# 32 of 48 blocks of modulations as row sums on VectorE, instead of float32 matmuls and products by feature tile

## The chip, the cores and the metric

One core of a Trainium2 chip runs the whole network. The metric is the device time of one execution in microseconds (us), the median of the runs shown.

## What is computed

Two residual layers over 256 latent and 256 context tokens of 1024 features. Layer 0 mixes tokens by neighbourhood attention and a gated linear recurrence (HGRN2), layer 1 by an SSD recurrence; each mixer is followed by a convolutional FFN of width 2816. What the change touches is the modulation: two vectors, `silu(c)` for the latent and `silu(c_ctx)` for the context tokens, times a 1024 x 6144 matrix in each layer.

```python
s_lat = jax.nn.silu(c)
s_ctx = jax.nn.silu(c_ctx)[None]
for l in range(DEPTH):
    sh_m, sc_m, g_m, sh_f, sc_f, g_f = jnp.split(s_lat @ w_mod[l] + b_mod[l], 6, axis=-1)
    csh_m, csc_m, cg_m, csh_f, csc_f, cg_f = jnp.split(s_ctx @ w_mod[l] + b_mod[l], 6, axis=-1)
    u = modulate(h, norm_mix[l], sh_m, sc_m)      # rms_norm * (1 + scale) + shift
    ...
    h = h + g_m[:, None] * y
    h = h + g_f[:, None] * conv_ffn(modulate(h, norm_ffn[l], sh_f, sc_f), ffn_w_up[l],
                                    ffn_conv_w[l], ffn_conv_b[l], ffn_w_down[l])
```

So per layer there are six chunks of 1024 columns: 0 shift and 1 scale of the mixer's norm, 2 the mixer's gate, 3 and 4 shift and scale of the FFN's norm, 5 the FFN's gate. Everything is float32.

## The kernel before

Features lie on partitions (8 tiles of 128), the 512 tokens on the free axis. Every large product is made of three float32r matmuls: `wsplit` (L127) loads a weight of 512 KB on SyncE's queue, ScalarE casts its high part (`whi`, L136) and VectorE subtracts it for the low part (`wlo`, L138), four buffers of each; `mm3` (L142, L145) multiplies high by low, high by high and low by high; `proj` and `proj_tm` (L147, L153) loop over the 8 feature tiles. A scheduler in the framework writes the order of each engine from the program order, the tiles and its own costs; each engine then runs its list strictly in order.

**Modulations.** The 2 x 6 x 1024 columns are made in 48 blocks of 256. `mod_load` (L168) fetches a block's 1 MB, `mod_block` (L173) multiplies it by both vectors in 8 float32 matmuls (16 records, L181), up to four blocks sharing a bank of PSUM; `mod_finish` (L190) copies the bank (`mrow`, L187), transposes it back to features on partitions (L193), adds up four column groups (L195), and `mod_store` (L198) adds the bias (L204) and, for scales, makes `A = (1 + scale) * gain` (L207). `bg` (L222) puts the next block into TensorE's stream between two projections; three blocks are loaded ahead.

16 of the 48 blocks take another way, within FFN 0: `vec_half` (L232) multiplies half a block, feature tile by feature tile, by a scalar per partition on VectorE and adds into `vacc` (L247, L249; 16 instructions of 128x256 for a block, 8 for each vector), and `vec_flush` (L256) has TensorE add up the partitions of four blocks with a ones-matmul (L264), ScalarE copy the sums (L267) and TensorE transpose them (L270).

**Where the blocks stand.** 8 at the start, for layer 0's first norm (L720, L731); 12 queued at L482 and put between the projections of the two HGRN pairs (L485, L500); one behind the attention (L766) and 3 in FFN 0's norm (`norm_mod`, L371); 16 on VectorE in FFN 0 (L420, L439); one late in FFN 0 (L441), 3 in layer 1's norm, one behind the SSD groups (L789), 3 in FFN 1's norm.

**Around the change.** `hybrid` (L714 on) starts with the projection of the first outputs, feature tile by feature tile, as modulations arrive: for tile k, VectorE normalises (`nt`, L364), ScalarE modulates and rounds (`xhi`, L366), VectorE makes the rest (`xlo`, L367). Meanwhile small parameters load on ScalarE's queue, among them `lbx` (L449), from which the bounds of the forget gates are made on VectorE (L451 to L461). `hgrn_pair` then projects the queries, forget gates and values of a pair of heads, and works through halving levels of its decay products on VectorE (L514), each with many small matmuls on TensorE (L536, into `attc` by L538 and L543). Pair 1's levels run beside the attention's first projections (L162 to L164).

Of the kernel before, what the change touches and what calls it, by code (L numbers as in the profile page):

```python
# [16 lines left out]
P = 128  # L17
# [9 lines left out]
BATCH = 4  # L27
# [7 lines left out]
def mod_cols(g, kt):  # L35
    """The two 128-column blocks of w_mod that block kt of group g makes."""
    if g == 0:
        return kt, 8 + kt
    if g == 2:
        return 24 + kt, 32 + kt  # L40
    i = (16 if kt < 4 else 40) + 2 * (kt % 4)
    return i, i + 1


class Net:
    def __init__(self, tc, ctx, ins, out):
# [32 lines left out]
        self.half, self.vdone = 0, None  # L79
# [11 lines left out]
    def act_set(self, n, after):  # L91
        """Loads a table set on the scalar engine, behind one of its instructions."""
# [23 lines left out]
    def open_psum(self, start):  # L116
        """Three banks: one for modulations and two at the start, shared later."""
# [8 lines left out]
    # ---------------------------------------------------------------- weights  # L126
# [39 lines left out]
    # ------------------------------------------------------------ modulations  # L166
    # groups: 0 shift and scale of the mixer, 1 the two gates, 2 shift and scale of the ffn
    def mod_load(self, l, g, k0, n, m, pool=None, bufs=3):  # L168
        w = (pool or self.w).tile([P, NK, 2 * P], F32, tag="wm", bufs=bufs, name=self.nm("wm"))
        self.nc.sync.dma_start(w, self.i["wmod"][l, g, k0 + m])  # L170
        return w, l, g, k0, n, m

    def mod_block(self, w, l, g, k0, n, m):  # L173
        """Block k0 + m of group g, the m-th of n that share a bank of PSUM; the last one finishes all n."""
# [4 lines left out]
        for k in range(NK):  # L179
            j = k % 4  # L180
            mm = nc.tensor.matmul(ps[32 * j:32 * j + 32, :2 * P], self.silu_c[:, k, 6 - 2 * m:38 - 2 * m], w[:, k, :],  # L181
                                  start=(m == 0 and k < 4), stop=(m == n - 1 and k >= 4))
# [28 lines left out]
    def queue(self, batches):  # L211
        self.pending += [(l, g, k0, BATCH, m) for l, g, k0 in batches for m in range(BATCH)]
        self.fetch()

    def fetch(self):
        while self.pending and len(self.loaded) < 3:
            self.loaded.append(self.mod_load(*self.pending.pop(0)))
# [14 lines left out]
    def vec_half(self, pool):  # L232
        """Half of a block's products on the vector engine; the tensor engine adds up the partitions of n blocks."""
        nc = self.nc
        self.vec_flush()
        if not self.loaded and not self.half:
            return
        if not self.half:
            self.vw = self.loaded.pop(0)
            if self.vw[-1] == 0:  # L240
                self.vacc = pool.tile([P, self.vw[-2], 2, 2 * P], F32, tag="vacc", bufs=1, name=self.nm("vacc"))
        w, l, g, k0, n, m = self.vw
        for k in range(4 * self.half, 4 * self.half + 4):
            for s in STREAMS:
                acc, sc = self.vacc[:, m, s], self.silu_c[:, k, 6 + s:7 + s]
                if k == 0:
                    nc.vector.tensor_scalar(out=acc, in0=w[:, k], scalar1=sc, scalar2=None, op0=ALU.mult)  # L247
                else:
                    nc.vector.scalar_tensor_tensor(out=acc, in0=w[:, k], scalar=sc, in1=acc, op0=ALU.mult, op1=ALU.add)  # L249
        if self.half:  # L250
            self.fetch()
            if m == n - 1:
                self.vdone = (self.vacc, l, g, k0, n, pool)
        self.half = 1 - self.half

    def vec_flush(self):  # L256
        if not self.vdone:
            return
        nc = self.nc
        acc, l, g, k0, n, pool = self.vdone  # L260
        self.vdone = None
        ps = self.ps_b()
        for m in range(n):
            nc.tensor.matmul(ps[32 * m:32 * m + 32], self.ones[:, :32], acc[:, m].rearrange("p s c -> p (s c)"),  # L264
                             start=True, stop=True)
        rows = pool.tile([P, T], F32, tag="vrow", bufs=1, name=self.nm("vrow"))
        nc.scalar.copy(rows, ps)  # L267
        pt = self.ps_b()
        for i in range(4):
            nc.tensor.transpose(pt[:, i * P:(i + 1) * P], rows[:, i * P:(i + 1) * P], self.ident)  # L270
        self.mod_store(cust(pt, 0, [[P, 2], [32, n], [2 * P, 2]]), l, g, k0, n)
# [4 lines left out]
    # ------------------------------------------------------------------- norm  # L276
# [4 lines left out]
    def rsqrt_few(self, y, x, n, pool):  # L281
        """y = 1 / sqrt(x / n + eps) for a few columns: Newton steps on the vector engine."""
# [12 lines left out]
    def sumsq(self, k, tok):  # L295
        """Adds the squares of feature tile k to the running sum over the features."""
# [12 lines left out]
    def norm_r(self, ps, t0, n, meanwhile):  # L309
        """1 / rms of each token, on every partition; the sums go to ps."""  # L310
# [24 lines left out]
    def first_norm(self, p, meanwhile):  # L335
        """Loads the tokens; 1 / rms of each, on every partition."""
# [20 lines left out]
    def norm_u(self, l, which, k, r, xhi, xlo, streams, pool):  # L357
        """Feature tile k of the modulated norm, in two parts."""
# [12 lines left out]
    def norm_mod(self, l, which, xhi, xlo, streams, pool):  # L371
        self.bg(1, self.last_mm)
        r = self.norm_r(self.ps_s(), S * streams[0], S * len(streams), lambda i: self.bg(1, i))
        self.vec_flush()
# [27 lines left out]
    # -------------------------------------------------------------------- ffn  # L402
# [715 lines left out]
```

## Time and profile before

| | |
|---|---|
| median of 3 runs | 1255.38 us (1254.75 to 1260.44) |
| profiled execution, first to last instruction (span) | 1254.5 us |
| time around the span, median less span | 0.9 us |
| mean granted TensorE clock | 0.998 |
| busy share: TensorE, VectorE, ScalarE | 98%, 70%, 47% |
| all transfers | 188 MB, 150 GB/s on average |

The page gives the profiled execution by its span alone. PE is TensorE, DVE VectorE, ACT ScalarE, SP SyncE. A line L181 is line 181 of the kernel before; the changed kernel has its own line numbers. "Idle before" is the time an engine stood before an instruction and what released it. Matmuls overlap on TensorE, so a group's busy time there is more than what it adds to the span.

### The profile page before, as it was taken

What the parts mean: (1) busy time and instruction counts of PE and PEld (TensorE: products, weight loads), DVE (VectorE), ACT (ScalarE), POOL (GpSimd) and SP (SyncE); (2) the same over time, 40 slices, a digit from 0 to 9 for tenths busy, and PEclk for the clock granted to TensorE, in tenths of its full rate; (3) what the DMA queues carried; (4) which work ended last, traced back from release to release, by engine and by line L of the source; (5) the groups of instructions that cost most, each with busy time, mean ns of one, the idle gap of its engine ahead of it and who ended that gap; (6) DMA issues with size and microseconds to landing.
All of it is one profiled execution on the core that took longest, in us unless ns stands there. A gap on an engine that the chain in (4) does not pass through costs nothing.

```text
span 1254.5 us, 19641 instructions
## 1 busy us (share of the span) xinstructions
PE 1225.9 (98%) x7827; PEld 991.1 (79%) x7827; DVE 874.7 (70%) x1599; ACT 589.3 (47%) x918; POOL 0.2 (0%) x4
## 2 busy tenths in 40 slices
PE   5899999999999999999999999999999999999998
PEld 4686787766677887887887887777777798999998
DVE  5558257477658969647849747688989786766665
ACT  4364434678645332233223335646473644645452
POOL 0000000000000000000000000000000000000000
PEclk9999999999999999999999999999999999999999
DMA  9744552223044544433634444445343345565663
GB/s 377 255 140 150 185 206 65 69 78 118 21 138 165 179 157 153 166 99 94 212 102 161 142 146 151 143 133 181 110 159 118 101 154 167 171 186 180 187 181 106
DMA packets 49195, 188.34 MB, mean 150 GB/s; under 512 B 6480, under 2 KB 10192, under 8 KB 42832
## 3 DMA queue, kind: packets, MB, share of 16 engines
q1 hardware_dynamic: 46224, 185.17, 44.4%
q10 hardware_dynamic: 2880, 1.92, 0.5%
q8 instruction: 61, 1.00, 0.3%
q14 instruction: 30, 0.25, 0.1%
HBM read 185.95 MB, written 1.11 MB: 149 GB/s over the span
## 4 chain that ended last, share of the span: by engine, by line
PE 92%; DVE 3%; DMA 2%; ACT 1%; issue 1%; ACTq 0%; SPq 0%; DVEq 0%
PE a L145 54%; PE s L145 17%; PE b L181 1%; PE b L699 1%; PE s L162 1%; PE s L163 1%; PE s L164 1%; PE b L998 1%; PE b L993 1%; PE s L679 1%; PE b L693 1%; PE s L680 1%; PE b L966 1%; PE b L931 1%; DMA bcB<-cum_scratch 1%
## 5 line engine op out<-in xcount | busy, mean ns | idle before, releaser
L136 ACT CAST whi<-raw 128x1024 fp32r<-128x1024 f32 (+1 forms) x234 | 240.8, 1032 | 363.0 <-PE a L145 281.8
L138 DVE TENSOR_TENSOR wlo<-raw,whi 128x1024 fp32r<-128x1024 f32 (+1 forms) x234 | 280.4, 1200 | 137.9 <-ACT whi L136 136.7
L145 PE MATMUL a<-xhi,wlo 128*128 128x512 f32 (+1 forms) x740 | 271.2, 371 | 0.6 <-ACT va L634 0.3
L145 PE MATMUL a<-xhi,whi 128*128 128x512 f32 (+1 forms) x740 | 271.0, 366 | 0.0
L145 PE MATMUL a<-xlo,whi 128*128 128x512 f32 (+1 forms) x740 | 258.1, 366 | 1.0 <-DVE xlo L367 1.0
L145 PEld LDWEIGHTS a<-xhi,wlo 128*128 128x128 f32 x740 | 138.9, 188 | 32.1 <-issue 6.0
L145 PEld LDWEIGHTS a<-xlo,whi 128*128 128x128 f32 x740 | 137.3, 188 | 28.9 <-issue 4.8
L145 PEld LDWEIGHTS a<-xhi,whi 128*128 128x128 f32 x740 | 139.3, 188 | 24.5 <-issue 2.9
L145 PE MATMUL s<-xhi,wlo 128*128 128x512 f32 (+1 forms) x376 | 128.5, 342 | 0.0
L145 PE MATMUL s<-xhi,whi 128*128 128x512 f32 (+1 forms) x376 | 128.0, 340 | 0.0
L145 PE MATMUL s<-xlo,whi 128*128 128x512 f32 (+1 forms) x376 | 121.9, 342 | 0.0
L145 PE MATMUL a<-hh,whi 128*128 128x256 f32 (+1 forms) x359 | 119.5, 333 | 0.0
L145 PE MATMUL a<-hh,wlo 128*128 128x256 f32 (+1 forms) x359 | 112.9, 334 | 0.0
L145 PE MATMUL a<-hl,whi 128*128 128x256 f32 (+1 forms) x359 | 111.7, 334 | 0.0
L249 DVE SCALAR_TENSOR_TENSOR vacc<-wm,silu_c,vacc 128x256 f32<-128x256 f32 x224 | 93.1, 477 | 0.0
L381 DVE SCALAR_TENSOR_TENSOR h<-a,modT,h 128x256 f32<-128x256 f32 x90 | 40.7, 480 | 62.5 <-PE a L145 62.5
L145 PEld LDWEIGHTS s<-xhi,wlo 128*128 128x128 f32 x376 | 70.6, 188 | 9.7 <-issue 0.4
L145 PEld LDWEIGHTS s<-xhi,whi 128*128 128x128 f32 x376 | 70.7, 188 | 9.1
L145 PEld LDWEIGHTS s<-xlo,whi 128*128 128x128 f32 x376 | 69.3, 188 | 9.1
L145 PEld LDWEIGHTS a<-hh,whi 128*128 128x128 f32 x359 | 68.2, 190 | 6.6
L145 PEld LDWEIGHTS a<-hh,wlo 128*128 128x128 f32 x359 | 66.6, 190 | 7.7 <-DVE t L424 0.8
L145 PEld LDWEIGHTS a<-hl,whi 128*128 128x128 f32 x359 | 66.3, 190 | 7.0
(340 smaller groups left out, 1827.6 us busy)
## 6 DMA issues: line engine op xcount, KB each, us to landing
wm<-in_wmod SPq DMA_DIRECT2D x48, 1024.0 KB, 5.6
raw<-in_wup SPq DMA_DIRECT2D x88, 512.0 KB, 4.1
raw<-in_win SPq DMA_DIRECT2D x41, 512.0 KB, 3.7
raw<-in_wdn SPq DMA_DIRECT2D x32, 448.0 KB, 3.3
raw<-in_wo SPq DMA_DIRECT2D x24, 512.0 KB, 3.7
raw<-in_wdn SPq DMA_DIRECT2D x16, 512.0 KB, 3.6
raw<-in_wz SPq DMA_DIRECT2D x16, 512.0 KB, 3.9
mix<-cum_scratch SPq DMA_DIRECT2D x8, 512.0 KB, 4.7
```

The costliest lines, as they stand in the source:

```text
L136: nc.scalar.copy(hi, raw)
L138: nc.vector.tensor_tensor(out=lo, in0=raw, in1=hi.bitcast(F32), op=ALU.subtract)
L145: self.last_mm = self.nc.tensor.matmul(ps, w, x, start=(first and i == 0), stop=(last and i == 2))
L162: mm(ps, xhi[:, k, tok], wlo[:, kk, :], start=(k == 0), stop=False)
L163: mm(ps, xhi[:, k, tok], whi[:, kk, :], start=False, stop=False)
L164: mm(ps, xlo[:, k, tok], whi[:, kk, :], start=False, stop=(k == NK - 1))
L181: mm = nc.tensor.matmul(ps[32 * j:32 * j + 32, :2 * P], self.silu_c[:, k, 6 - 2 * m:38 - 2 * m], w[:, k, :], start=(m == 0 and k < 4), sto ...
L249: nc.vector.scalar_tensor_tensor(out=acc, in0=w[:, k], scalar=sc, in1=acc, op0=ALU.mult, op1=ALU.add)
L381: self.nc.vector.scalar_tensor_tensor(out=self.h[:, n, s * S:(s + 1) * S], in0=ps[:, off:off + S], scalar=self.mod(l, chunk, n, s), in1=se ...
L679: nc.tensor.matmul(ps, qs[rows, e, tok], kl[rows, :w], start=True, stop=False)
L680: nc.tensor.matmul(ps, qs[:, e, tok], ks[:, e, :w], start=False, stop=True)
L693: nc.tensor.transpose(pt[:, b * P:(b + 1) * P], pr[:, b * P:(b + 1) * P], self.ident)
```

## The change

32 blocks (64 units of 128 features) are made on VectorE as row sums. The host lays `w_mod` out a second time as `wmodT`, one output feature to a partition and its 1024 weights along the free axis, and gives `crow`, both vectors as one row. `vec_start` broadcasts that row to all partitions (1 MB, ScalarE's queue) and applies SILU to it once. A unit is a 512 KB load and two `scalar_tensor_tensor` of 128x1024, one per vector, with a running sum that lands in one column of `dots`; the elementwise product goes to `junk`. After 8 units, a bias addition and, for scales, the product with the gains finish 1024 features, with no TensorE work and no transpose. `vec` stands where `bg` stood in the HGRN pairs and the attention, and in FFN 0 once for each hidden tile and each output tile; at two places (L769, and L1028 behind FFN 0) it takes what is left. On TensorE remain the 8 blocks of the start and the 8 of layer 1's gates, in the norms of FFN 0, layer 1 and FFN 1 (3, 3 and 2), loaded one ahead and in two halves.

```diff
-    def vec_half(self, pool):
-    def vec_flush(self):
+    def vec_start(self):
+        nc = self.nc
+        self.rows = self.const.tile([P, 2, NK * P], F32, name="rows")
+        self.junk = self.const.tile([P, NK * P], F32, name="junk")
+        src = self.i["crow"].rearrange("s k -> (s k)").unsqueeze(0).to_broadcast([P, 2 * NK * P])
+        nc.scalar.dma_start(self.rows.rearrange("p s k -> p (s k)"), src)
+        nc.scalar.activation(self.rows, self.rows, AF.Silu)
...
+    def vec_fetch(self):
+        while self.units and len(self.fetched) < 3:
+            l, c, k = self.units.pop(0)
+            w = self.w.tile([P, NK * P], F32, tag="wv", bufs=5, name=self.nm("wv"))
+            self.nc.sync.dma_start(w, self.i["wmodT"][l, 8 * c + k])
+            self.fetched.append((w, l, c, k))
...
+    def vec(self, n=1):
...
             for s in STREAMS:
+                nc.vector.scalar_tensor_tensor(out=self.junk, in0=w, scalar=1.0, in1=self.rows[:, s], op0=ALU.mult,
+                                               op1=ALU.mult, accum_out=self.dots[:, k, s:s + 1])
+            self.vec_fetch()
+            if k < NK - 1:
+                continue
+            dst = self.modT[:, l, 8 * c:8 * c + 8, :]
+            nc.vector.tensor_tensor(out=dst, in0=self.dots, op=ALU.add,
+                                    in1=cust(self.bmod[:, l, 8 * c:8 * c + 1], 0, [[1, 8], [0, 2]]))
...
-                        self.queue([(0, 1, 0), (0, 2, 0), (0, 2, 4)])
+                        self.vec_queue([(0, 3), (0, 4), (0, 2)])
...
-                    self.bg()
+                    self.vec()
...
-        self.bg(2)
+        self.vec(2)
...
                 self.load_params()
+                self.vec_start()
...
-            self.bg(16)
-            self.flush()
-            self.queue([(1, 0, 0), (0, 1, 4), (1, 0, 4), (1, 2, 0), (1, 2, 4), (1, 1, 0), (1, 1, 4)])
-            self.bg(1)
+            self.vec(NK * 3)
+            self.vec_queue([(0, 5), (1, 0), (1, 1), (1, 3), (1, 4)])
+            self.queue([(1, 1, 0, 3), (1, 1, 3, 1), (1, 1, 4, 2), (1, 1, 6, 2)])
...
-                    for _ in range(0 if last else (0, 0, 1, 1, 1, 1, 2, 2)[f] if f < 8 else 1):
-                        self.vec_half(self.vec)
+                    if not last:
+                        self.vec(1)
...
-                    if not last and m % 2 == 0 and m < (8, 8, 4)[c]:
-                        self.vec_half(self.vec)
-                    if not last and c == 2 and m == 4:
-                        self.bg(1)
+                    if not last:
+                        self.vec(1)
```

The change moves instructions on every engine, as the scheduler writes their order anew. Below are the places at which it matters most; `wv` is a unit's weights, `dots` its sums, and numbers behind names count buffers.

ScalarE at the start, before: the load of `lbx` stands ahead of a weight's cast and of the rounding of two feature tiles (`nt_408`).

```order
L62 DMA c_sconv<-in_sconv 128x96
L741 DMA id_564<-in_id 128x32
L743 DMA blk_566<-in_blk 128x128
L449 DMA lbx<-in_hg_lb 128x24
L136 CAST whi_393<-raw_391 128x896
L454 ACTIVATE lbx<-lbx 128x24
L366 ACTIVATE xhi<-nt_408,modT 128x256 x2
```

ScalarE at the start, now:

```order
L61 DMA c_sconv<-in_sconv 128x96
L245 DMA rows<-in_crow 128x2048
L135 CAST whi_393<-raw_391 128x896
L747 DMA id_568<-in_id 128x32
L749 DMA blk_570<-in_blk 128x128
L246 ACT_TABLE_LOAD
L246 ACTIVATE rows<-rows 128x2048
L376 ACTIVATE xhi<-nt_408,modT 128x256 x2
```

The load of `rows` and the SILU over it stand there instead, with a table load, ahead of `nt_408`; `lbx` is loaded four instructions later.

VectorE at the start, before: the first use of `lbx` stands ahead of the split of a weight and of `mrow_355`, the modulations that `nt_408` waits for.

```order
L752 COPY qkg<-c_small 128x1
L451 TENSOR_TENSOR lbm<-lbx 128x8
L138 TENSOR_TENSOR wlo_394<-raw_391,whi_393 128x896
L187 COPY mrow_355<-m_302 128x256
L452 TENSOR_TENSOR lbm<-lbm,lbx 128x8
L453 TENSOR_TENSOR lbx<-lbx,lbm 128x24
L457 TENSOR_TENSOR lbo<-lbx 128x8
L195 TENSOR_REDUCE mres_359<-m_302 128x2x4
```

VectorE at the start, now:

```order
L758 COPY qkg<-c_small 128x1
L137 TENSOR_TENSOR wlo_394<-raw_391,whi_393 128x896
L193 COPY mrow_355<-m_302 128x256
L201 TENSOR_REDUCE mres_359<-m_302 128x2x4
L210 TENSOR_TENSOR modT<-mres_359,c_bmod 128x2x4
L213 SCALAR_TENSOR_TENSOR A<-modT,c_gains 128x4
L374 SCALAR_TENSOR_TENSOR nt_408<-h,A,fr_173 128x256 x2
```

The small instructions on `lbx` and its products have gone from here. They come later, mixed with the first four row sums, ahead of the norm of the next pair of tiles (`nt_494`):

```order
L137 TENSOR_TENSOR wlo_525<-raw_522,whi_524 128x896
L269 SCALAR_TENSOR_TENSOR junk,dots_660<-wv_623,rows 128x1024
L193 COPY mrow_452<-m_399 128x256
L462 TENSOR_TENSOR lbo<-lbx 128x8
L269 SCALAR_TENSOR_TENSOR junk,dots_660<-wv_623,rows 128x1024
L201 TENSOR_REDUCE mres_456<-m_399 128x2x4
L463 TENSOR_TENSOR lbm<-lbo,lbx 128x8
L269 SCALAR_TENSOR_TENSOR junk,dots_660<-wv_625,rows 128x1024
L210 TENSOR_TENSOR modT<-mres_456,c_bmod 128x2x4
L464 RECIPROCAL lbm<-lbm 128x8
L213 SCALAR_TENSOR_TENSOR A<-modT,c_gains 128x4
L269 SCALAR_TENSOR_TENSOR junk,dots_660<-wv_625,rows 128x1024
```

Three of the four row sums and `lbo` stand between `mrow_452` and `nt_494`, where nothing but three small instructions stood.

VectorE ahead of pair 1's levels, before: `attc` by L538 is their first instruction.

```order
L540 TENSOR_TENSOR Q_1209<-h,f_1211 128x1024
L524 TENSOR_TENSOR kc_1708<-K_1210 128x1024
L514 TENSOR_TENSOR K_1210<-K_1210,f_1211 128x512 x2
L514 TENSOR_TENSOR f_1211<-f_1211 128x512
L138 TENSOR_TENSOR wlo_2182<-raw_2179,whi_2181 128x1024
L138 TENSOR_TENSOR wlo_2212<-raw_2209,whi_2211 128x1024
L195 TENSOR_REDUCE mres_1698<-b_1473 128x16
L538 TENSOR_TENSOR attc_1707<-b_1710,id_564 128x256
```

VectorE there, now (`attc` by L543):

```order
L545 TENSOR_TENSOR Q_1195<-h,f_1197 128x1024
L529 TENSOR_TENSOR kc_1627<-K_1196 128x1024
L137 TENSOR_TENSOR wlo_2071<-raw_2068,whi_2070 128x1024
L519 TENSOR_TENSOR K_1196<-K_1196,f_1197 128x512 x2
L137 TENSOR_TENSOR wlo_2101<-raw_2098,whi_2100 128x1024
L519 TENSOR_TENSOR f_1197<-f_1197 128x512
L269 SCALAR_TENSOR_TENSOR junk,dots_2211<-wv_2164,rows 128x1024
L269 SCALAR_TENSOR_TENSOR junk,dots_2211<-wv_2168,rows 128x1024 x2
L269 SCALAR_TENSOR_TENSOR junk,dots_2211<-wv_2214,rows 128x1024
L543 TENSOR_TENSOR attc_1626<-b_1629,id_568 128x256
```

Four row sums have come in directly ahead of `attc`, and the finish of a bank of modulations (L195) has gone. In all, 39 row sums stand between the start and `attc`, 15 between the levels and the attention, none from there to FFN 0, and 74 in FFN 0 up to the twelfth hidden tile. In FFN 0 VectorE's list reads, before:

```order
L249 SCALAR_TENSOR_TENSOR vacc_3891<-wm_3978,silu_c,vacc_3891 128x256 x4
L424 TENSOR_TENSOR t_4058<-t_4058,s_3989 128x512
L249 SCALAR_TENSOR_TENSOR vacc_3891<-wm_3978,silu_c,vacc_3891 128x256
L138 TENSOR_TENSOR wlo_4181<-raw_4178,whi_4180 128x1024
L389 TENSOR_TENSOR hl_3682<-t_4058,hh_3681 128x512
L249 SCALAR_TENSOR_TENSOR vacc_3891<-wm_3978,silu_c,vacc_3891 128x256 x9
L138 TENSOR_TENSOR wlo_4239<-raw_4236,whi_4238 128x1024
```

and now:

```order
L137 TENSOR_TENSOR wlo_4694<-raw_4691,whi_4693 128x1024
L406 SCALAR_TENSOR_TENSOR t_4607<-a_4540,c_fconv,t_4607 128x2x255
L275 TENSOR_TENSOR modT<-dots_5125,c_bmod 128x16
L269 SCALAR_TENSOR_TENSOR junk,dots_5473<-wv_5298,rows 128x1024
L408 SCALAR_TENSOR_TENSOR t_4607<-a_4540,c_fconv,t_4607 128x2x255
L269 SCALAR_TENSOR_TENSOR junk,dots_5473<-wv_5298,rows 128x1024
L433 TENSOR_TENSOR t_4607<-t_4607,s_4541 128x512
L137 TENSOR_TENSOR wlo_4724<-raw_4721,whi_4723 128x1024
L398 TENSOR_TENSOR hl_4539<-t_4607,hh_4538 128x512
```

The products by feature tile (L247, L249), in runs of up to nine, are replaced by row sums in runs of one or two between the splits of weights and the convolution (`t`).

## Rows read from the trace of the kernel before

**Rows 1.** The page, parts 1 and 4: span, busy times, the chain by engine

```profile
span 1254.5 us, 19641 instructions
...
PE 1225.9 (98%) x7827; PEld 991.1 (79%) x7827; DVE 874.7 (70%) x1599; ACT 589.3 (47%) x918; POOL 0.2 (0%) x4
...
PE 92%; DVE 3%; DMA 2%; ACT 1%; issue 1%; ACTq 0%; SPq 0%; DVEq 0%
```

**Rows 2.** Busy times by window (us; engines PE, PEld, DVE, ACT, POOL; clock; DMA share)

```profile
64.00:185.00 121.00, 118.33 (x1324) 92.71 (x1323) 67.25 (x116) 58.29 (x88) 0.00 (x0) 1.00 0.49 168
185.00:209.00 24.00, 23.38 (x431) 17.44 (x424) 23.70 (x51) 8.80 (x16) 0.00 (x0) 1.00 0.29 98
209.00:227.00 18.00, 17.71 (x95) 14.03 (x94) 6.42 (x16) 9.76 (x15) 0.00 (x0) 1.00 0.12 41
395.00:562.00 167.00, 167.00 (x728) 134.33 (x727) 123.71 (x227) 56.53 (x69) 0.00 (x0) 1.00 0.44 145
```

**Rows 3.** Groups of instructions by line, 395 to 562 us (busy us, mean ns | idle before)

```profile
L249 DVE SCALAR_TENSOR_TENSOR vacc<-wm,silu_c,vacc 128x256 f32<-128x256 f32 x112 | 46.1, 477 | 0.0
...
L247 DVE TENSOR_SCALAR vacc<-wm,silu_c 128x256 f32<-128x256 f32 x16 | 5.2, 345 | 0.0
```

**Rows 4.** The chain that ended last, 0 to 82 us: start us, us, what

```profile
35.66 8.55 DMA lbx<-in_hg_lb
...
46.49 2.13 PE a L145 x5
...
51.60 1.00 PE m L181 x16
```

**Rows 5.** Timelines of VectorE and of TensorE, 38 to 60 us; idle before in brackets

```profile
44.24 0.17 DVE L451 TENSOR_TENSOR lbm<-lbx 128x8 f32<-128x8 f32 x1 [8.13 <-DMA lbx<-in_hg_lb]
...
45.80 0.69 PE L193 MATMUL m<-c_ident,mrow 128*128 128x128 f32 x2 [4.29 <-DVE mrow L187]
```

**Rows 6.** The chain that ended last, 82 to 230 us

```profile
143.00 5.80 PE a L145 x24
...
183.63 0.44 PE b L193 x2
```

**Rows 7.** Groups by form, whole span; then line 977 (ns, min/median/max)

```profile
L942 DVE TENSOR_TENSOR mix<-mix,alpha 128x1024 f32<-128x1024 f32 x8 | 9.8, 1222 | 0.5 <-DMA mix<-cum_scratch 0.5
...
L944 ACT ACTIVATE mix<-mix 128x2048 f32<-128x2048 f32 x4 | 7.7, 1918 | 1.8 <-DVE mix L943 1.8
...
L990 DVE TENSOR_TENSOR h<-xt,coef 128x512 f32<-128x512 f32 x8 | 5.5, 687 | 0.0
...
L977 DVE SCALAR_TENSOR_TENSOR dg<-cb,c_ident x8: 281/290/312, 833.6 to 1005.3; 128x128 f32<-128x128 f32 x8
L977 DVE DVE_READ_ACCUMULATOR dg<-cb,c_ident x8: 80/82/109, 833.8 to 1005.6; 128x1 f32 x8
```

**Rows 8.** Timeline of VectorE, 176 to 230 us

```profile
184.61 0.41 DVE L538 TENSOR_TENSOR attc<-b,id 128x256 f32<-128x256 f32 x1
...
185.56 1.28 DVE L514 TENSOR_TENSOR Q<-Q,f 128x512 f32<-128x512 f32 x2
```

**Rows 9.** DMA issues: KB each, us to landing; the page, then 0 to 82 us

```profile
mix<-cum_scratch SPq DMA_DIRECT2D x8, 512.0 KB, 4.7
...
raw<-in_win SPq DMA_DIRECT2D x8, 448.0 KB, 10.5
```

**Rows 10.** Groups of instructions by line, 82 to 230 us

```profile
L181 PE MATMUL b<-wm,silu_c 128*32 128x256 f32 x176 | 11.4, 384 | 0.0
```

**Rows 11.** The chain that ended last, later windows

```profile
347.69 0.99 PE b L181 x14
...
474.84 0.99 PE b L264 x8
...
477.20 0.44 PE b L270 x4
...
742.04 1.00 PE b L181 x16
```

More of the change, by code (lines that the diff above doesn't have):

```diff
@@ L211, in queue @@
     def queue(self, batches):
-        self.pending += [(l, g, k0, BATCH, m) for l, g, k0 in batches for m in range(BATCH)]
+        self.pending += [(l, g, k0, n, m) for l, g, k0, n in batches for m in range(n)]
         self.fetch()
     def fetch(self):
-        while self.pending and len(self.loaded) < 3:
+        while self.pending and not self.loaded:
             self.loaded.append(self.mod_load(*self.pending.pop(0)))
@@ L230, in bg @@
                 self.fetch()
-    def vec_half(self, pool):
+    def vec_start(self):
         nc = self.nc
[L235 to L243, printed above, removed]
-            for s in STREAMS:
[L245 to L254, printed above, removed]
@@ L256, in vec_flush @@
-    def vec_flush(self):
[L257 to L271, printed above, removed]
+        self.rows = self.const.tile([P, 2, NK * P], F32, name="rows")
@@ new lines, in vec @@
+    def vec(self, n=1):
+        nc = self.nc
+        for _ in range(n):
+            if not self.fetched:
+                return
+            w, l, c, k = self.fetched.pop(0)
+            if k == 0:
+                self.dots = self.w.tile([P, NK, 2], F32, tag="dots", bufs=2, name=self.nm("dots"))
+            for s in STREAMS:
+                nc.vector.scalar_tensor_tensor(out=self.junk, in0=w, scalar=1.0, in1=self.rows[:, s], op0=ALU.mult,
+                                               op1=ALU.mult, accum_out=self.dots[:, k, s:s + 1])
+            self.vec_fetch()
+            if k < NK - 1:
[3 more added lines that the diff above has]
+                                    in1=cust(self.bmod[:, l, 8 * c:8 * c + 1], 0, [[1, 8], [0, 2]]))
+            if c in (1, 4):
+                which = (c - 1) // 3
+                nc.vector.scalar_tensor_tensor(
+                    out=self.A[:, l, which], in0=dst, scalar=1.0, op0=ALU.add, op1=ALU.mult,
+                    in1=cust(self.gains[:, 2 * which + l, 0:1], 0, [[1, NK], [0, 2]]))
@@ L425, in ffn @@
                     self.split_to(hh[:, j, :], hl[:, j, :], t)
-                if c == 0 and not last:
-                    self.vec_flush()
                 for m in range(NK):
@@ L631, in attention @@
         self.proj_tm(pv, [self.i["wv0"][b] for b in range(4)], xhi, xlo, range(4), 512)
-        self.bg(3)
+        self.vec(3)
         for tt in range(4):
```

39 lines of the change are left out of this document (24 added, 15 removed).

## Prediction

> **What bounds the kernel now.** The page comes first: TensorE is busy 98% of the span and 92% of the chain that ended last is its own, against 3% for VectorE and 2% for transfers; VectorE is busy 70% [rows 1]. So a matmul taken off TensorE should shorten the run, as long as the engine that gets its work has room at that place. The windows show where VectorE has room [rows 2]: in the 121 us of the projections of the two HGRN pairs it works 67.25 us, in the halving levels of pair 1 (185 to 209 us) 23.70 of 24, between them and the attention (209 to 227 us) 6.42 of 18, and in the first 167 us of FFN 0 123.71, of which 46.1 + 5.2 are today's products by feature tile [rows 3]. The chain of the start, read with the timelines, shows one further hole: VectorE stands 8.13 us for the load of `lbx` (issued at 35.66, 8.55 us under way), and the copy of `mrow` behind it lets TensorE idle 4.29 us; five matmuls behind that take 2.13 us, 0.43 each, where 24 usually take 5.80, 0.24 each [rows 4, 5, 6].
>
> The sums are made against the profiled span, 1254.5 us [rows 1]. The median of the runs is 1255.38, so 0.9 us lie outside the span and are added at the end.
>
> **The price of a row sum.** The trace has no 128x1024 product with a running sum. A 128x1024 product of two float32 operands takes 1.22 us and a 128x512 one 0.69 [rows 7]: 1.04 ns an element over some 0.16 fixed. The one instruction with `accum_out`, on 128x128, takes 0.290, which that line gives too (0.16 + 0.13), and a read of the accumulator of 0.082 follows it [rows 7]. Instructions in a row overlap by 0.1 us (two of 0.69 take 1.28 together [rows 8]), so the bounds are 1.12 (overlap, read hidden) and 1.34 (1.22 + 0.08 and a gap of 0.04). I take **1.25**, a little above the middle, since the read is an instruction of its own that shows in the rows. 128 of them are 160 us of VectorE.
>
> The Trainium skill speaks against this ("Vector Engine (DVE) Microarchitecture Reference", the points that are easy to get wrong): a scalar_tensor_tensor with two SBUF sources that are not bf16 takes both read ports and runs at half rate. By that a row sum would be some 2.3 us, an estimate from the element rate above. The rows do not bear it out: the 128x128 form with two float32 sources runs at 0.290, not at about 0.42. It stays as a rival below.
>
> **The start.** The load of `lbx` moves behind the casts, and VectorE's first use of it behind three weight splits; TensorE's transposes no longer wait for it. What takes its place is ScalarE's SILU over `rows`, a 1 MB broadcast issued where `lbx` was (about 34.7), which stands before the casts of feature tiles 4 and 5. Its landing is unknown. Below, the 512 KB broadcasts of layer 1 take 4.7 us; above, the weights loaded in this stretch take 10.5 [rows 9]. I take 8.6, `lbx`'s own [rows 4], as it was issued by the same engine at the same place. Then `rows` is there at 43.3; a 128x2048 activation is 1.92 us [rows 7], so 45.2, and with cast, split and weights tile 4's matmuls start at about 46.9, where tile 3's end when nothing holds them. Today they start at 52.6, behind the block at 51.60 [rows 4]: **5.7 us** earlier. Three row sums that stand between `mrow` and the norm of tile 6 give back up to 3.8; some of it is slack that a tile's 5.6 us of matmuls leave, and I book 1.6. Start: **+4.1**, with 2.1 if the load takes 10.5 and a loss of 1 if it needs another 3 beyond that.
>
> **Layer 0's mixer.** Twelve blocks leave TensorE there: one just ahead of 82 us and eleven (176 records, 16 to a block) up to 230 [rows 10], at the 1.00 that a block takes on the chain [rows 4], and three pairs of transposes of 0.44 [rows 6]: 12 x 1.0 + 1.3 = 13.3. On TensorE's side alone pair 1's levels could start at 184.6 - 4.1 - 13.3, about 167. But VectorE now has 35 row sums between the start and these levels (39 in the order less four of the start), 35 x 1.25 = 43.75 on top of 67.25 [rows 2]: 111 us from about 61, full, and the levels' first instruction (now at 184.61 [rows 8]) comes at **172.5**. So VectorE becomes what sets it: 12.1 us earlier, not 17.4. The levels themselves stay as long, as VectorE fills them now. Nine row sums stand behind, where 11.6 us are free for 11.3: I book 0.6 for the chances that one stands ahead of a product that is waited for, and 0.9 for four more filler matmuls that the order leaves for the stretch behind. At 226.9 the kernel is **10.5 us** ahead, the start's 4.1 among them.
>
> Queues: SyncE issues 512 KB loads of `wmodT` where it issued 1 MB blocks, the same bytes; a row sum's buffer is one of five and it runs at most three ahead, so a weight could wait behind a buffer not yet free. Today no weight of this stretch is late by its own transfer, and I cost it at nothing; the cover is the four buffers of split weights, worth three products of 5.8 us [rows 6].
>
> **Everything later.** No block at 345 to 349 us, where 0.99 of it is one piece of the chain [rows 11] and a first piece and its transposes another 0.5: +1.5. Three of the four flushes by ones-matmuls go off TensorE's path at 0.99 + 0.44 each [rows 11], +4.3; the fourth falls with a norm's waits and is left at nothing. Two blocks that stood alone in TensorE's stream (at 742 us, 1.00 [rows 11], and one behind the SSD groups) +2.0; the norms of layer 1 and of FFN 1 with a block fewer +0.8; the norm of FFN 0 gives back 0.3, as its loads come only one ahead. Together **+8.3**.
>
> FFN 0 must hide the other 74 row sums: 123.7 - 51.3 + 92.5 = 164.9 us of VectorE in the 167 us in which today's products stand [rows 2, 3]. This is full. What saves it is that the order puts the row sums behind the weight splits, and that splits run up to three products (17 us) ahead. I cost it at nothing; without that cover each 0.01 us on the price is 0.7 us.
>
> **Sum:** 10.5 + 8.3 = 18.8 off 1254.5, 1235.7; with 0.9, **1236**.
>
> **Rivals.**
> - *VectorE does not pack.* The order is right only if no row sum stands ahead of something that TensorE waits for. At 98% of VectorE in two stretches of 110 and 165 us, a loss of 5 to 10% of the first, 5 to 11 us, is no surprise: 1242 to 1249. For it: in the stretch of the levels, where VectorE is full today, TensorE has holes. Against: with splits three ahead, lateness is caught up where TensorE works on long products. 0.16.
> - *Row sums are cheap* (1.12, or the order's slack is larger): the mixer gains TensorE's whole 13, the FFN has 8 us to spare: 1226 to 1231. 0.09.
> - *The load of `rows` holds ScalarE.* 1 MB through one queue, among 1 MB blocks; if it lands after 47, the start's gain is gone, and part of the mixer's with it: 1243 to 1252. 0.07.
> - *Slower: a row sum at half rate.* The place is VectorE in the mixer and in FFN 0, the price 1.05 more for each: the levels 35 x 1.05 + 3.2 later, 40; nine row sums of 20.7 into 11.6 us, 10 with what they hold; FFN 0 78 less its 17 of cover, 61; less the 18.8: about +92, some 1345. It decides from about 1.55 us a row sum (then 35 x 0.3 + 0.9 and 22 - 17 = 16.4 eat nearly all); below that the change still wins. The 128x128 form speaks against it, and no row shows one that is long. 0.05.
> - *The change does not do what it says.* Blocks that stay on TensorE, or row sums bunched behind the FFN: the order has no block on TensorE between the start and FFN 0's norm, and no row sum behind FFN 0's second third. Only that SyncE's loads are late remains, with TensorE waiting at a norm for a scale: 1249 to 1262. 0.05.
>
> **How the numbers follow.** The forecast's own case (1230 to 1243, from 1.20 to 1.30 us a row sum and 2 to 5.7 us at the start) has 0.58; the rivals above have the rest. The range reaches into the first two: **1228 to 1247**, leaving out the half-rate case, most of the last one, and pieces of both edges. About 0.5% (6.3 us) is what a measurement of this kernel can tell from no change, so under 1249 is faster: nearly all of the forecast, of the first two rivals and half of the third, 0.85. Within 0.5%: 0.09. Slower: the half-rate case and a part of the last, 0.06.
>
> **What would show it.** Row sums of 1.2 to 1.35 us; `rows` landing near 43 and ScalarE's SILU behind it; no wait for `lbx` on VectorE; VectorE without idle time from 62 us to the levels' start, and that start near 172; TensorE without holes in FFN 0; no `m`, `b` or `vacc` rows of blocks on TensorE outside the start and the three norms. I am wrong where a row sum is over 1.35 us, where the levels start after 180, or where TensorE idles in FFN 0 with VectorE's splits as the releaser.

## The result, and the profile after

The change takes 1234.7 us (median of 4 runs, 1233.98 to 1236.18) beside 1257.47 us for the kernel before on the same chip (4 runs, 1254.75 to 1260.44): a ratio of 0.9824, 95% interval 0.9805 to 0.9843. The profiled execution is the 1236.18 us one, with a span of 1234.4 us; so 1.8 us lie around the span, where 0.9 had been taken; the other executions measured here have 1.7 to 1.9 as well. Between the two profiled spans the gain is 20.1 us.

The kernel after, the page, parts 1 and 4 (beside [rows 1]):

```profile
span 1234.4 us, 19131 instructions
...
PE 1205.3 (98%) x7519; PEld 981.4 (80%) x7519; DVE 924.7 (75%) x1596; ACT 589.8 (48%) x915; POOL 0.2 (0%) x4
...
PE 85%; DVE 6%; issue 2%; ACT 1%; DMA 0%; DVEq 0%; ACTq 0%
```

TensorE has lost 308 matmuls and 20.6 us of busy time; VectorE has gained 50.0 us of busy time and 5 points of share. The product by tiles is replaced by these groups (groups by form; busy us, mean ns | idle before):

```profile
L269 DVE SCALAR_TENSOR_TENSOR junk<-wv,rows 128x1024 f32<-128x1024 f32 x128 | 156.2, 1221 | 1.9
...
L269 DVE DVE_READ_ACCUMULATOR junk<-wv,rows 128x1 f32 x128 | 10.5, 82 | 0.0
```

A row sum takes 1.22 us, the time of the plain 128x1024 product in [rows 7], and its read 0.08. How they follow each other is in VectorE's timeline just ahead of pair 1's levels, whose first instruction is `attc`:

```profile
163.14 0.69 DVE L519 TENSOR_TENSOR f<-f 128x512 f32<-128x512 f32 x1
163.74 1.22 DVE L269 SCALAR_TENSOR_TENSOR junk<-wv,rows 128x1024 f32<-128x1024 f32 x1
164.88 0.08 DVE L269 DVE_READ_ACCUMULATOR junk<-wv,rows 128x1 f32 x1
165.00 1.23 DVE L269 SCALAR_TENSOR_TENSOR junk<-wv,rows 128x1024 f32<-128x1024 f32 x1
...
168.69 0.42 DVE L543 TENSOR_TENSOR attc<-b,id 128x256 f32<-128x256 f32 x1
```

The read starts 0.08 before the row sum's end. A second row sum begins 1.26 behind the first; where another instruction follows at once, that one mostly begins 1.14 to 1.15 behind. The 35 row sums between 61 and 168.7 us occupied 41.7 us with their reads, 1.19 each, where 1.25 was booked.

The windows that answer to [rows 2] (PE, PEld, DVE, ACT, POOL; clock; DMA share, GB/s): the projections, the levels of pair 1, the stretch up to the attention's first product, and FFN 0 in two parts:

```profile
61.00:168.70 107.70, 105.88 (x1130) 88.08 (x1131) 105.55 (x186) 56.83 (x86) 0.00 (x0) 1.00 0.51 163
168.70:193.00 24.30, 23.64 (x424) 17.47 (x423) 24.04 (x51) 8.73 (x16) 0.00 (x0) 1.00 0.19 61
193.00:211.80 18.80, 16.86 (x92) 13.23 (x90) 18.44 (x37) 10.33 (x16) 0.00 (x0) 1.00 0.63 181
380.00:545.00 165.00, 165.00 (x709) 132.59 (x708) 158.23 (x247) 55.47 (x68) 0.00 (x0) 1.00 0.67 208
545.00:700.00 155.00, 155.00 (x666) 124.56 (x665) 70.27 (x91) 48.70 (x60) 0.00 (x0) 1.00 0.33 99
```

VectorE is full in all but the last, as forecast, and TensorE has no hole in FFN 0. But the levels begin at 168.69, not at 172.5. On TensorE the first products of the levels, which `attc` reads, end at 167.19, 1.5 us earlier (timeline of TensorE):

```profile
166.43 0.76 PE L541 MATMUL b<-h,kc 128*32 128x32 f32 x64
```

Where the 20.1 us come from, read at the same instruction of both timelines (before, after, gain):

| place | before | after | gain |
|---|---|---|---|
| pair 0's levels, first `attc` | 94.45 | 90.18 | 4.3 |
| pair 1's levels | 184.61 | 168.69 | 15.9 |
| attention's first product | 226.87 | 211.79 | 15.1 |
| transposes in FFN 0's norm | 381.92 | 367.21 | 14.7 |
| norm of layer 1 | 761.39 | 744.20 | 17.2 |
| norm of FFN 1 | 1059.88 | 1041.79 | 18.1 |
| end | 1254.5 | 1234.4 | 20.1 |

So 15.1 us are there at the attention (10.5 forecast) and 5.0 come later (8.3 forecast).

**The start.** `rows` landed in 6.1 us, where 8.6 had been taken (DMA issues, 0 to 82 us: KB, us to landing):

```profile
rows<-in_crow ACTq DMA_DIRECT2D x1, 1024.0 KB, 6.1
...
lbx<-in_hg_lb ACTq DMA_DIRECT2D x1, 12.0 KB, 6.9
```

VectorE still waits for `lbx`, but 3.36 us instead of 8.13 [rows 5], and TensorE's next transposes wait 1.16 instead of 4.29 (timelines of VectorE and TensorE):

```profile
52.19 0.17 DVE L456 TENSOR_TENSOR lbm<-lbx 128x8 f32<-128x8 f32 x1 [3.36 <-DMA lbx<-in_hg_lb]
...
55.33 0.44 PE L199 MATMUL m<-c_ident,mrow 128*128 128x128 f32 x2 [1.16 <-DVE mrow L193]
```

**A wait and a slow stretch at the attention.** TensorE stands 1.94 us for `va`, and its products soon take 0.63 us where 0.39 is usual (timeline of TensorE):

```profile
211.79 0.50 PE L144 MATMUL a<-xhi,wlo 128*128 128x512 f32 x1 [1.94 <-ACT va L639]
...
214.11 0.63 PE L144 MATMUL a<-xhi,wlo 128*128 128x512 f32 x1
```

The windows there show the granted clock at 0.50, the lower of its two levels, after TensorE had worked only 1.06 of 3 us:

```profile
209.00:212.00 3.00, 1.06 (x5) 0.59 (x4) 2.82 (x6) 2.97 (x5) 0.00 (x0) 1.00 0.41 132
213.00:214.00 1.00, 1.00 (x4) 0.81 (x4) 1.00 (x2) 0.98 (x2) 0.00 (x0) 0.66 0.91 297
214.00:215.00 1.00, 1.00 (x4) 0.71 (x4) 0.96 (x3) 0.50 (x1) 0.00 (x0) 0.50 0.92 240
```

It lasts 3.4 us and costs 1.7: the gain of 15.1 is 13.6 at TensorE's next products for a norm (234.21 before, 220.66 after).

### The profile page after: what moved, and what is told of

It reads as the page before. It is cut to its first block, busy times and chain, and to the rows that moved or that the text cites. A ratio compares the mean times of both kernels' runs of the same rounds, so it can differ in the third digit from the quotient of the medians.

```text
span 1234.4 us, 19131 instructions
## 1 busy us (share of the span) xinstructions
PE 1205.3 (98%) x7519; PEld 981.4 (80%) x7519; DVE 924.7 (75%) x1596; ACT 589.8 (48%) x915; POOL 0.2 (0%) x4
## 4 chain that ended last, share of the span: by engine, by line
PE 85%; DVE 6%; issue 2%; ACT 1%; DMA 0%; DVEq 0%; ACTq 0%
PE a L144 51%; PE s L144 16%; PE b L704 1%; PE s L161 1%; PE s L162 1%; PE s L163 1%; DVE junk L269 1%; PE b L997 1%; PE b L970 1%; PE b L1002 1%; DVE Q L519 1%; PE s L684 1%; PE b L698 1%; PE s L685 1%; DVE K L519 1%
## 5 line engine op out<-in xcount | busy, mean ns | idle before, releaser
L144 PEld LDWEIGHTS a<-xlo,whi 128*128 128x128 f32 x740 | 137.4, 188 | 31.5 <-issue 4.6
L269 DVE SCALAR_TENSOR_TENSOR junk<-wv,rows 128x1024 f32<-128x1024 f32 x128 | 156.2, 1221 | 1.9
```

The lines of the kernel that those rows point to most:

```text
L144: self.last_mm = self.nc.tensor.matmul(ps, w, x, start=(first and i == 0), stop=(last and i == 2))
L269: nc.vector.scalar_tensor_tensor(out=self.junk, in0=w, scalar=1.0, in1=self.rows[:, s], op0=ALU.mult, op1=ALU.mult, accum_out=self.dots[:, ...
```

## The experiments

Each is an edit of the changed kernel unless another is named; ratios are to the kernel before, run beside it on the same chip. `attc` is the first instruction of pair 1's levels.

### Put the twelve mixer blocks back on TensorE

```diff
-                        self.vec_queue([(0, 3), (0, 4), (0, 2)])
+                        self.queue([(0, 1, 0, 4), (0, 2, 0, 4), (0, 2, 4, 4)])
...
-                    self.vec()
+                    self.bg()
```

> The changed kernel, but the 12 blocks of layer 0's mixer are float32 matmuls on TensorE again; the other 40 units (80 row sums) all stand in FFN 0. My account (the start gives about 4 us by itself, TensorE sets the mixer again, the later 5 us stay): pair 0's levels start near 90 us, the attention's first product near 221 to 223 us (226.9 before, 211.8 with the change), time 1242 to 1247. Rival one (the start gives nothing by itself): attention at 226, 1249 to 1251. Rival two (80 row sums do not hide in FFN 0): TensorE has idle time there with VectorE's splits as releaser, over 1250.

Measured: 1254.03 us, ratio 0.9963 (0.995 to 0.9976). A miss, and a confounded one. With nothing else queued for VectorE in the mixer, the scheduler moved six row sums meant for FFN 0 ahead of pair 1's levels, and one waits for its weights (timeline of VectorE):

```profile
167.58 1.23 DVE L269 SCALAR_TENSOR_TENSOR junk<-wv,rows 128x1024 f32<-128x1024 f32 x1 [5.10 <-DMA wv<-in_wmodT]
```

`attc` comes at 182.17 and the attention's first products wait 3.7 us for `va`. The run says nothing on the blocks alone, but it shows that a row sum whose weights are late can hold VectorE for 5.10 us.

The same with the row sums queued only behind FFN 0's norm, and TensorE's blocks loaded two ahead:

```diff
+            if not last: self.vec_queue([(0, 5), (1, 0), (1, 1), (1, 3), (1, 4)])
...
-        while self.pending and not self.loaded:
+        while self.pending and len(self.loaded) < (2 if self.pending[0][0] == 0 else 1):
```

> As e1_mixer_pe, but the row sums' loads start only behind FFN 0's norm, so that none of the 80 row sums stands in the mixer, and TensorE's blocks stand where they stood before the change. My account: start as in the changed kernel (pair 0's levels near 89 to 90 us, 94.45 before), then TensorE sets the mixer: pair 1's levels start 177 to 180 (184.61 before, 168.69 with the change), the attention's first product 219 to 222; the later pieces keep the changed kernel's 5 us: 1242 to 1246. Rival (the mixer's 12 blocks cost little by themselves and most of the gain is the start's): attention by 216, time 1236 to 1240.

Measured: 1244.41 us, ratio 0.9918 (0.9903 to 0.9933), span 1242.3, as expected. The timelines of VectorE and TensorE:

```profile
177.91 0.41 DVE L543 TENSOR_TENSOR attc<-b,id 128x256 f32<-128x256 f32 x1
...
220.18 0.51 PE L144 MATMUL a<-xhi,wlo 128*128 128x512 f32 x1 [0.29 <-ACT va L639]
```

Without the twelve blocks' move the attention starts at 220.18. Of the 15.1 us there, the start gives 6.7 and the blocks 8.4; the blocks are worth 7.9 by the profiled spans and some 12 by the ratios to the kernel before (0.9918 and 0.9824, on two chips).

### Load `lbx` first, in both kernels

```diff
+        self.lbx = c.tile([P, 2, 3, 4], F32, name="lbx"); nc.scalar.dma_start(self.lbx, ins["hg_lb"])
         self.ident = load("ident", [P, P])
...
-        x = p.tile([P, 2, 3, 4], F32, name="lbx")
-        nc.scalar.dma_start(x, self.i["hg_lb"])
+        x = self.lbx
```

In the kernel before:

> The kernel before, but lbx is the first load of ScalarE's queue, so that VectorE does not wait for it at 36 to 44 us. My account: TensorE's 4.3 us hole and the half clock behind it go, and as TensorE sets the mixer in this kernel all of it carries to the end: 5 to 6 us less than before, 1249.5 to 1252. Rival (the next wait of the start takes its place, or the mixer's slack swallows it): within 1.5 us of before.

Measured: 1250.94 us, ratio 0.995 (0.9929 to 0.997), span 1249.0. VectorE has no wait for `lbx` any more; the copy of `mrow` comes at 40.93. Pair 0's levels start at 89.04 (5.4 earlier), the attention's products at 219.34 (7.5 earlier), and 5.5 are left at the end of the span. So the hole at the start was real, and could be closed without the rest of the change.

In the changed kernel:

> The changed kernel with the same early load of lbx. VectorE stands 3.4 us for lbx at 52 us in the changed kernel. My account: as VectorE sets the start of pair 1's levels there, 1 to 3 us of these carry on: 1231.5 to 1234. Rival (VectorE waits for the next modulations instead): within 0.7 us of the changed kernel.

Measured: 1233.57 us, ratio 0.9806 (0.979 to 0.9822); `attc` at 166.15 instead of 168.69, and the median of the spans is 1231.8 beside 1232.9 in the change. About 1 us, at the edge of what can be told.

### Make each row sum dearer, or most of the mixer's nearly free

A copy of 128x256 behind each row sum, which adds 31.5 us to VectorE's busy time, 0.25 for each:

```diff
+                nc.vector.tensor_copy(self.junk[:, 0:256], w[:, 0:256])
```

> The changed kernel with a 128x256 copy behind every row sum, about 0.35 us more for each. My account (VectorE sets the start of pair 1's levels): 35 of them make these levels start 11 to 13 us later, near 181 (168.7 with the change), the attention's first product comes 13 to 16 us later, and FFN 0 (158 us of VectorE in 165, now some 26 more, 17 us of cover by splits made ahead) lets TensorE idle 0 to 10 us: 1247 to 1257. Rival (TensorE sets the levels' start, VectorE has slack): levels by 172, time 1234 to 1239.

Measured: 1235.06 us, ratio 0.9815 (0.98 to 0.9829). My account fell. `attc` comes at 165.76, earlier than in the change. The trace has 31 row sums ahead of the levels where the change has 39, 23 between them and FFN 0 where it has 15, and 74 in FFN 0 as in the change, but 15 of these start behind 545 us where the change has one. The windows:

```profile
61.00:165.80 104.80, 103.78 (x1122) 86.39 (x1122) 103.09 (x193) 56.52 (x86) 0.00 (x0) 1.00 0.46 148
380.00:545.00 165.00, 165.00 (x710) 132.88 (x709) 158.22 (x275) 55.30 (x66) 0.00 (x0) 1.00 0.59 188
545.00:700.00 155.00, 155.00 (x666) 124.57 (x665) 89.52 (x135) 49.61 (x61) 0.00 (x0) 1.00 0.40 119
```

VectorE is as full as in the change up to the levels (98%) and up to 545 us, and takes 19 us more behind.

From the other side, the 24 units of layer 0's mixer summed over 64 of 1024 weights, the rest of these sums left out:

```diff
+                z = 64 if l == 0 and c < 5 else NK * P
-                nc.vector.scalar_tensor_tensor(out=self.junk, in0=w, scalar=1.0, in1=self.rows[:, s], op0=ALU.mult,
+                nc.vector.scalar_tensor_tensor(out=self.junk[:, :z], in0=w[:, :z], scalar=1.0, in1=self.rows[:, s, :z], op0=ALU.mult,
```

> The changed kernel, but the 24 units of layer 0 made in the mixer are summed over 64 of their 1024 weights (the rest of these sums is left out), which frees some 40 us of VectorE ahead of the attention. Theory one (VectorE alone sets the start of pair 1's levels): this start moves by 10 us or more, below 159. Theory two (TensorE is as full: 105.9 of 107.7 us): it moves by 1 to 4 us, to 165 to 168, and the time is 1230.5 to 1234.

Measured: 1233.25 us, ratio 0.9825 (0.9808 to 0.9842). The window and VectorE's timeline:

```profile
61.00:165.00 104.00, 100.85 (x986) 83.55 (x985) 78.49 (x201) 53.04 (x80) 0.00 (x0) 1.00 0.59 207
```

```profile
166.34 0.42 DVE L543 TENSOR_TENSOR attc<-b,id 128x256 f32<-128x256 f32 x1 [3.85 <-PE b L541]
```

With 25.5 us of VectorE free in 104, the levels start 2.4 us earlier than in the change, and VectorE waits there for TensorE, which is busy 100.85 of 104. The scheduler rewrote TensorE's order here too, so the two kernels differ in more than the sums; but with the 1.5 us read in the change's own trace it says the same: TensorE's own work sets that start to within 2.4 us, and VectorE's row sums add no more than that.

Then a copy of 128x1024 behind each row sum, meant to bring it to the 2.3 us of the half-rate rival:

```diff
+                nc.vector.tensor_copy(self.junk, w)
```

> The changed kernel with a 128x1024 copy behind every row sum, so that one takes about 2.3 us of VectorE, the price of the slower case of the prediction. That case, as written there (order of the instructions kept): the levels 40 us late, FFN 0 over by 61, some 1320 to 1345. My account after the 128x256 copies cost nothing (the scheduler puts only as many row sums ahead of the levels as fit, and the second half of FFN 0 has 85 us free on VectorE): 26 row sums ahead of the levels, these start 165 to 172, and the time is 1236 to 1262, lost where FFN 0 or layer 1's norm waits for the last sums.

Measured: 1252.46 us, ratio 0.9987 (0.9971 to 1.0003), span 1249.6. The copy is cheaper than meant (timeline of VectorE):

```profile
163.54 0.69 DVE L270 COPY junk<-wv 128x1024 f32<-128x1024 f32 x1
```

The 128 copies add 77.5 us to VectorE's busy time, so a row sum with its copy takes about 1.8 us, not 2.3, and the rival's price itself was not tried. By the rival's own working 1.8 us would give 22 at the levels, 5 behind them and 24 in FFN 0, less the 18.8: 32 us slower than before, near 1287. The measured 1252.46 is some 35 below that. The scheduler puts 26 row sums ahead of the levels, which start at 167.62, and FFN 0 still hides its 74 (windows):

```profile
212.00:350.00 138.00, 130.16 (x538) 85.00 (x540) 115.20 (x240) 88.29 (x184) 0.00 (x0) 0.94 0.32 107
...
540.00:700.00 160.00, 160.00 (x687) 128.59 (x686) 130.42 (x194) 50.64 (x62) 0.00 (x0) 1.00 0.46 150
```

The loss is in the attention, where 28 row sums now stand between the levels and FFN 0 and TensorE works 130.16 of 138 us at a clock of 0.94. In the change it works nearly all of the same window:

```profile
212.00:350.00 138.00, 137.78 (x599) 92.13 (x599) 99.21 (x204) 96.73 (x195) 0.00 (x0) 0.99 0.30 95
```

Its waits with the copies (212 to 400 us; us in total, times, longest):

```profile
PE a L144 <- ACT va L639: 3.7, 1, 3.7
PE b L698 <- DVE pr L695: 2.0, 3, 1.3
PE s L684 <- ACT pr L693: 1.9, 4, 0.7
```

FFN 0's norm comes at 382.62, 0.7 later than in the kernel before: the mixer's whole gain is gone, and what is kept comes later.

### What FFN 0 gave back: the matmuls' step

By the n-th matmul of each timeline the down projections of FFN 0 lost 3.0 us against the kernel before, with no wait. One step lasts longer (chains of waits, 40 us of the first down projection, the kernel before and then after):

```profile
481.98 40.18 PE a L145 x177
```

```profile
465.95 40.14 PE a L144 x172
```

That is 227.0 and 233.4 ns a step. The instructions are the same; the tiles' addresses differ, since one buffer pool has gone. First test: unused tiles bring the pools' tiles back to the addresses that they had before, though the weights' buffers move too (from byte 88416 to 92384).

```diff
+        self.pad = self.w.tile([P, 992], F32, name="pad")
...
+            if not last: p.tile([P, 2560], F32, name="padf")
```

> The changed kernel with every instruction in its place, but unused tiles shift the pools so that the operands of the attention's output, of the FFNs' and of layer 1's output lie at the SBUF addresses that they had before the change. In the trace of the changed kernel a matmul of 512 columns in FFN 0's output projections takes 233.3 ns from start to start, 226.7 before. Theory one (the place of the operands sets it): 226.7 again in the three stretches, 3 us less, and FFN 1, which became 1.4 us quicker, gives that back; span 1230 to 1232.5. Theory two (the row sums' traffic or the mix of instructions sets it): 233.3 stays and the span is that of the changed kernel, 1232.2 to 1234.4.

Measured: 1237.75 us, ratio 0.9868 (0.985 to 0.9885): a miss. FFN 0's down step is still 232.4 ns, and the up step has grown too (chain):

```profile
402.86 5.63 PE a L144 x24
...
464.90 40.21 PE a L144 x173
```

It isn't the address of the other operand by itself. But for one cell of the table below, the steps of all kernels so far sort by another quantity, the distance in bytes from the weights' buffers to the other operand, modulo 512, by the addresses that the kernels' buffers get. The next kernel sets it in three places, the down projections of both FFNs and the SSD's output:

```diff
+            p.tile([P, 40 if last else 96], F32, name="padf")
...
+            p.tile([P, 96], F32, name="pads")
```

> The changed kernel, every instruction in its place; unused tiles of 384, 384 and 160 bytes a partition shift the operands of FFN 0's output projections, of layer 1's output projection and of FFN 1's, so that their distance to the weights' buffers is, modulo 512 bytes, what it was where the trace of before has the short steps (0 for 512 columns, 288 for 256 columns), though their addresses are others. Theory one (that distance modulo 512 sets a matmul's step): 226.7 ns instead of 233.3 in FFN 0's output projections (528 matmuls, 3 to 3.5 us), near 117 instead of 119 to 120 in the other two (1 to 2 us): 4 to 5.5 us under the changed kernel, 1229 to 1231.5. Theory two (the absolute addresses of before matter, or something else): steps and time stay, 1234 to 1236.

Measured: 1231.35 us, ratio 0.9781 (0.9759 to 0.9803). The chain in FFN 0's down projection is back at 227.0:

```profile
464.88 40.18 PE a L144 x177
```

With 72 more floats among the weights' buffers, the distance of the normed tokens (`xhi`, `xlo`) is 0 as well:

```diff
+        self.pad = self.w.tile([P, 72], F32, name="pad")
```

> As e9_pads, and the weights' buffers moved by 288 bytes, so that the distance to the normed tokens (xhi, xlo) is a multiple of 512 too, at which the 512-column matmuls of FFN 0's input projections (1056), of the mixer's and of layer 1's projections should take 226.7 instead of 233.3 ns by theory one: 7 us in FFN 0 and 2 to 3 in the rest; FFN 1's input projections (1056 of 256 columns) leave the distance 288 and should go from about 117 to 120, 3 us back. Net 5 to 8 us under e9_pads: 1222 to 1226. Theory two: no step changes, the time is that of e9_pads.

Measured: 1223.42 us, ratio 0.9726 (0.9702 to 0.9749). The chains of FFN 0's and FFN 1's up projections:

```profile
404.72 5.44 PE s L144 x24
...
1111.49 2.88 PE s L144 x24
```

In the change the same 24 steps take 5.60 and 2.80. So 0 is the best of the distances tried for 512 columns, and a bad one for 256. In ns per step, with the distance in brackets:

| projection, columns | before | change | addresses back | three places | and `xhi`, `xlo` |
|---|---|---|---|---|---|
| FFN 0 up, 512 | 233.3 (288) | 233.3 (288) | 234.3 (416) | | 226.7 (0) |
| FFN 0 down, 512 | 227.0 (0) | 233.4 (128) | 232.4 (128) | 227.0 (0) | 226.7 (0) |
| SSD output, 256 | 117.2 (288) | 120.0 (416) | 117.3 (416) | 116.7 (288) | 116.7 (288) |
| FFN 1 up, 256 | | 116.7 (288) | | | 120.0 (0) |
| FFN 1 down, 256 | 120.0 (0) | 118.7 (128) | | 116.7 (288) | 116.7 (288) |

One cell spoils the order (SSD output with the addresses back, 117.3 at 416, where the change has 120.0), so the distance isn't the whole rule; only 0, 128, 288 and 416 came up. More runs say so of this product (chains of TensorE, 48 steps of it: the change, the same kernel run again, the change with copies of 128x1024, whose buffers lie at the same places):

```profile
1015.23 5.76 PE s L144 x48
```

```profile
1014.02 5.70 PE s L144 x48
```

```profile
1030.57 5.63 PE s L144 x48
```

That is 120.0, 118.7 and 117.3 ns a step at one distance and the same addresses, so at 416 something else moves it, and what was not found. The steps of 512 columns don't vary so: 233.3 in FFN 0's up projections in the change and in its second run.

### The best of it, and the change again

Distance 0 for all products of 512 columns, 288 for those of 256 in FFN 1 and the SSD's output (FFN 1's normed tokens in tiles of their own), and `lbx` loaded first:

```diff
+            if last: xhi, xlo, toks = [p.tile([P, NK, S], F32R, name=q) for q in ("xh1", "xl1")] + [slice(0, S)]
...
+            p.tile([P, 120], F32, name="padn")
```

> e10_pads_x with three more edits: lbx loaded first (1 us, as in e4_lbx_after), the attention's output at distance 0 to the weights (96 matmuls, 0.6 us), and FFN 1's normed tokens in tiles of their own at distance 288 instead of 0 (1056 matmuls from 120 back to 116.7 ns, 3 us). By the distance theory 1218 to 1220.5; if FFN 1's matmuls stay at 120 or its norm gets a new wait from the new tiles, 1221 to 1223.

Measured: 1219.91 us (5 runs, 1218.8 to 1220.94), ratio 0.969 (0.9674 to 0.9706). Both up steps are short now (chain):

```profile
406.82 5.44 PE s L144 x24
...
1111.58 2.80 PE s L144 x24
```

> The changed kernel as it is, on the same chip as e11_best: 1233 to 1237, levels of pair 1 at 168.7, 233.3 ns a matmul in FFN 0; the half-clock stretch behind the attention's wait may or may not appear in the profile, worth 1.7 us.

Measured, on the same chip: 1234.97 us, ratio 0.9816 (0.9798 to 0.9834), span 1232.9. Its profile has no half-clock stretch behind the attention's start, though TensorE waits 1.94 us there as well: of the seven profiles with that wait (1.93 to 1.94 us), three show the stretch (the change's first, the kernel with three places set and the best one). The best kernel is 15.1 us faster than the change, 39.3 than the kernel before.

## Why the prediction was right, and where not

1236 was forecast (1235.7 and 0.9 are 1236.6) and 1234.7 measured. That it came so close is in part luck: two terms were off in opposite directions, 4.6 us too little gain at the attention and 3.3 too much behind it, with 0.9 too little around the span.

- **The price of a row sum: right within its bounds.** It is mostly 1.14 to 1.27 from start to start, 1.19 on average ahead of the levels, where I took 1.25. The read of the accumulator lies in the shadow of the next instruction unless that writes `junk` too: another row sum, or the copy in the run with 128x256 copies, begins 1.26 to 1.27 behind. The rule of the Trainium skill that I weighed ("Vector Engine (DVE) Microarchitecture Reference", the points that are easy to get wrong) is not borne out: 1219 ns is the median for two float32 sources in SBUF, no longer than a plain product of that size.
- **The start: right.** 4.3 us at pair 0's levels for 4.1. Two assumptions in it were off: the load of `rows` (6.1 for 8.6), and `lbx`, which VectorE still waits for. By the attention the start is worth 6.7 (the run with the mixer's blocks put back); why it grows by 2.4 on the way was not tried.
- **"So VectorE becomes what sets it", 172.5: the step that failed.** It took the order's 39 row sums as fixed, and multiplied. For this order the sum was 3.8 us too long: 2.0 is the price (41.7 for 43.75), 3.4 VectorE's other work in the window (63.8 for 67.25), less 2.2 us of idle time, and 0.5 lies between 61 + 111 and the 172.5. In the change's trace VectorE is indeed last at `attc`, but by 1.5 us only, not by the 5.5 of the forecast. And the runs show that it isn't VectorE's load that sets the place: whether a row sum takes next to nothing or 1.8 us, `attc` stays between 165.8 and 168.7, and the number of row sums ahead of it goes from 54 to 26. That the scheduler fits VectorE's list to the time that TensorE leaves is how I read these counts. That a full VectorE stood in the window was true, and no proof that it bounds. TensorE's side alone, forecast for 167, is ready at 167.2.
- **The stretch up to the attention: too cheap, and one thing missed.** 18.8 us where 18 stood, within the 1.5 booked; ten row sums stand there for the nine that I counted. But TensorE waits 1.94 there, and in the profiled execution the clock falls behind it, 1.7 us that no term had.
- **FFN 0: right, for a better reason than mine.** No TensorE wait. I called it full at 164.9 of 167, with splits ahead as the only cover; its second half has VectorE busy 70.27 of 155, and that is where dearer row sums go. So the working of the slower rival was wrong, though its price was not tried: "it decides from about 1.55 us", but at about 1.45 nothing is lost, and at about 1.8, where that working gives +32, the kernel is level with the one before (0.9987, up to 1.0003), with the loss at the attention.
- **Everything later: 5.0 for 8.3.** The block at 345 (1.2 for 1.5), the flushes (4.7 for 4.3), the norm of FFN 0 (-0.3 for -0.3) and the two lone blocks (2.3 for 2.0) came as forecast. Unforecast were the matmuls' longer steps, -3.0 in FFN 0's down projections and -0.7 in the SSD's output, against +1.5 in FFN 1, and the 1.7 at the lower clock. The remaining 1.0 stands beside 0.8 booked for the norms.

## What to carry to other kernels

Where a scheduler writes the order, filler work has no fixed place: price a dearer or cheaper filler by the room that is left in all stretches where it may go, and test whether a full engine bounds by making its work lighter. Compare the matmul step of unchanged loops before and after any change of pools: a few ns over thousands of steps were worth more here than most terms of the sum. And read the first wait of each queue: moving one 12 KB load ahead was worth 0.5% by itself in the kernel before.

## What the runs showed that was not expected

- **The step of a float32r product depends on where its operands lie.** 226.7 to 234.3 ns for 512 columns and 116.7 to 120.0 for 256, for the same instructions at the same clock; setting it by unused tiles took the ratio to the kernel before from 0.9824 to 0.9726. For the SSD's output the same addresses gave 117.3 to 120.0, so there the address is not all of it. The Trainium skill ("TensorE: Matmul & The Clock Gate", Part 2: What happens when you issue a matmul) says that loading the next tile's weights takes no read bandwidth from the running matmul. These runs show a step that moves with the operands' addresses; whether reads get in each other's way, or something else, is open.
- **The clock fell behind a wait of less than 2 us, in one execution and not in the next of the same kernel**: 1.94 us of waiting in the profiled run of the change, then 3.4 us at 0.50; the same wait in its second run, and the clock at 1.00 throughout.
